# Attention scores as three 64-row terms, the two halves of the keys on the two halves of the rows

## The chip, the cores and the metric

The kernel runs on one core of one Trainium2 chip. The metric is the device time of one execution in microseconds (us). The kernel before takes 1475.3 us, the median of three runs (1474.57 to 1476.85).

## The reference, cut to what matters

Two encoder layers over 1024 tokens of width 1024. In each layer a normalised `x` is projected into two groups of heads: group A is differential attention (4 heads, each with two score maps over 64-wide queries and keys, and a relative-position bias), group B is grouped-query attention (8 query heads on 2 key heads, 64 wide, normalised and rotated). Each group's output is gated, both are concatenated, projected, normalised and added to `x`.

```python
sc = jnp.einsum('cbhqd,cbhkd->cbhqk', qblk, kt).astype(jnp.float32) + bias   # group A, d = 64
p = jax.nn.softmax(sc, axis=-1)
a = p[0] - lam * p[1]
...
sc = jnp.einsum('bgrqd,bgkd->bgrqk', qblk, kt).astype(jnp.float32)           # group B, d = 64
p = jax.nn.softmax(sc, axis=-1).astype(vt.dtype)
```

All values are float32. Every score is a sum over 64 products.

## The kernel before, in words

**Precision.** The matmuls work on float32 tiles of a rounded type (`F32R`). To keep float32 accuracy an operand is split into a rounded part, hi, and the rest, lo, and products are summed: hi·hi, hi·lo and lo·hi in the projections (`mm3`), and in the scores all four products.

**Stages of a layer.** First come the projections (from the start to 312 us in the first layer), which leave queries, keys and values, split, in DRAM tensors (`aq_d`, `ak_d`, `av_d`, `bq_d`, `bk_d`, `bv_d`). Then the attention stage (312 to 627 us in the first layer, 1041 to 1356 us in the second), then the output projection and the normalisation, which in the first layer runs on into the next layer's projections.

**The attention stage.** `all_items` goes through 4 head pairs `h` and 4 token groups `g`; each of these 16 steps has 8 items, 4 of group A and 4 of group B, so 128 items a layer and 256 in all. One item is 128 queries against 1024 keys. `tick` issues one item's work: transposes of an earlier item's probabilities (`pT`, 8 of 128 x 128), the reduction of this item's scores (DVE), the scores of the next item into a tile `pS` of 128 x 1024 (`scores`), some matmuls of probabilities with values (`pO`), the exponential (ACT), then what splits the transposed probabilities into hi and lo. In this stage all four engines execute in the order in which the program is written. `pS` and `pT` have two buffers each.

**The scores.** Rows 0 to 63 of a query tile and of a key tile hold 64 features, and so do rows 64 to 127. For group A the key tile has hi in the upper rows and lo in the lower, and the query tile has the same part in both, so that one matmul over 128 rows gives q·(hi + lo); a second matmul with the queries' lo part adds the other two products. For group B the queries' hi and lo are stacked and the keys doubled. Either way an item has four matmuls: two terms, each on two halves of 512 keys, since a matmul writes 512 columns:

```python
for i in range(2):
    x0 = qi * 512 + i * 256 + c * P
    for kh in range(2):
        n = slice(kh * 512, kh * 512 + 512)
        pe.matmul(pS[:, n], q[:, x0:x0 + P], K[:, c, n], start=(i == 0), stop=(i == 1))
```

**The loads of the stage.** SyncE (SP) issues every DMA, in order. `load_q` fetches the queries of one step (lines 803 to 808), `load_ak` keys of group A and a bias tile (810 to 818), `load_av` values, `load_bk` keys of group B. Their tiles, named `h`, come from a ring of ten buffers, so that a load waits on the SP queue until the tile ten allocations earlier has been read. The queries of a step are requested one step ahead.

**Elsewhere.** `build_bias_rows`, once in the first layer's projections, has the program's only matmuls on 64 rows (`pl[:4]`, 64 rows, 4 stationary columns, 512 columns; named `pO<-e,rbs` in the profile). They run in two visits of two, between projection matmuls into `pS`. Every compute instruction goes through a helper class, so the profile shows them all under its line, L65, and they are told apart by their tiles.

Of the kernel before, what the change touches and what calls it, by code (L numbers as in the profile page):

```python
# [10 lines left out]
F32R = mybir.dt.float32r  # L11
# [6 lines left out]
P = 128  # L18
S = 1024
# [32 lines left out]
def hybrid_encoder(ctx, tc, x, rel_bias, pre_norm_g, w_in, diff_lambda, diff_subln_g,  # L52
                   q_norm_g, k_norm_g, w_out, post_norm_g, onehot, rope, out):
    nc = tc.nc
# [16 lines left out]
    pe, dve, act, gps = Engine(nc.tensor), Engine(nc.vector), Engine(nc.scalar), Engine(nc.gpsimd)  # L71
# [11 lines left out]
    def nm(p):  # L83
        uid[0] += 1
        return f"{p}{uid[0]}"

    def h_tile(shape, dt=F32):
        return sb.tile(shape, dt, tag="h", name=nm("h"), bufs=10)
# [4 lines left out]
    def e_tile(shape=(P, 1024), dt=F32):  # L93
        return sb.tile(list(shape), dt, tag="e", name=nm("e"), bufs=6)
# [7 lines left out]
    def s_tile(n=1, tag="s", bufs=12):  # L102
        return sm.tile([P, n], F32, tag=f"{tag}{n}", name=nm("s"), bufs=bufs)

    def ps_s(shape=(P, 1024), dt=F32):
        return ps.tile(list(shape), dt, tag="S", name=nm("pS"), bufs=2)
# [7 lines left out]
    def d_tile(shape, name):  # L114
        return dr.tile(shape, F32, tag=name, name=name)

    def f(t):
        return t.bitcast(F32)
# [184 lines left out]
    def layer(l, hT, ends, given):  # L303
# [3 lines left out]
        aq_d = d_tile([4, 64, 4, 1024], f"aq_d{l}")  # L307
        ak_d = d_tile([4, 2, P, S], f"ak_d{l}")
        av_d = d_tile([4, P, 2, NT, P], f"av_d{l}")
        bq_d = d_tile([4, P, 4, 512], f"bq_d{l}")  # L310
        bk_d = d_tile([P, 2, 2, S], f"bk_d{l}")
# [275 lines left out]
        def after(delay, fn, mid=False):  # L587
            later_q.append((now[0] + delay, mid, fn))
# [8 lines left out]
        def transpose_unit(e, aT, qi, pool_half):  # L597
            c0 = qi * P
            rest = []
            for kh in range(2):  # L600
                pT = ps_t((P, 4, P))
                for i in range(4):
                    k = kh * 4 + i
                    pe.transpose(pT[:, i, :], e[:, k * P:(k + 1) * P], ident)
                hi = aT[0][:, kh * 4:kh * 4 + 4, c0:c0 + P]
                lo = aT[1][:, kh * 4:kh * 4 + 4, c0:c0 + P]
                if kh == pool_half:
                    full = e[:, kh * 512:kh * 512 + 512].rearrange("p (k c) -> p k c", c=P)
                    act.copy(full, pT)

                    def fin(hi=hi, lo=lo, full=full):
                        gps.tensor_copy(hi, full)
                        gps.tensor_tensor(lo, full, f(hi), ALU.subtract)
                else:
                    act.copy(hi, pT)

                    def fin(hi=hi, lo=lo, pT=pT):
                        dve.tensor_tensor(lo, pT, f(hi), ALU.subtract)
                rest.append(fin)
            return rest  # L620

        def tick(item, nxt):
# [17 lines left out]
            run_later(False)  # L640
            now[0] += 1

        def a_items(q, K, T5, t, qi, aT, r0, out):
            bias = T5[:, 896 - P * t:896 - P * t + 1024]
            es = [None, None]
            sums = s_tile(2, "asum", 4)
            items = []
            for c in range(2):
                def scores(c=c, box=[]):
                    pS = ps_s()  # L650
                    for i in range(2):
                        x0 = qi * 512 + i * 256 + c * P
                        for kh in range(2):
                            n = slice(kh * 512, kh * 512 + 512)
                            pe.matmul(pS[:, n], q[:, x0:x0 + P], K[:, c, n], start=(i == 0), stop=(i == 1))
                    return pS

                def reduce(pS, c=c):
                    es[c] = e_tile()
                    m = s_tile()  # L660
                    dve.tensor_tensor_reduce(out=es[c], in0=pS, in1=bias, op0=ALU.add, op1=ALU.min,
                                             scale=1.0, scalar=3.0e38, accum_out=m)
                    return m

                def expo(pS, m, c=c):
                    act.activation(es[c], es[c], AF.Exp, bias=m, scale=-1.0, accum_out=sums[:, c:c + 1])
                    if c == 1:
                        after(CD, combine)
                items.append((scores, reduce, expo))

            def combine():
                rec = s_tile(2, "arec", 4)
                dve.reciprocal(rec, sums)
                cc = s_tile()
                dve.scalar_tensor_tensor(cc, sums[:, 0:1], neglam, rec[:, 1:2], ALU.mult, ALU.mult)
                dve.tensor_copy(r0[:, qi:qi + 1], rec[:, 0:1])
                a, b = es
                gps.tensor_scalar(b, b, cc, 0.0, ALU.mult, ALU.add)
                gps.tensor_tensor(a, a, b, ALU.add)

                def go():
                    return transpose_unit(a, aT, qi, None) + [lambda: parts.extend(out or [])]
                trans.append((now[0] + AD, go))
            return items
# [44 lines left out]

        def b_items(q, K, j, qi, bT, sr, out):  # L730
            es = []

            def scores():
                pS = ps_s()
                x0 = 1024 + j * 256 + qi * P
                for i in range(2):
                    for kh in range(2):
                        n = slice(kh * 512, kh * 512 + 512)
                        pe.matmul(pS[:, n], q[:, x0:x0 + P], K[:, i, n], start=(i == 0), stop=(i == 1))
                return pS  # L740

            def reduce(pS):
                m = s_tile()
                dve.tensor_reduce(out=m, in_=pS, axis=AX.X, op=ALU.max, negate=True)
                return m

            def expo(pS, m):
                e = e_tile()
                act.activation(e, pS, AF.Exp, bias=m, scale=1.0, accum_out=sr[:, j * 2 + qi:j * 2 + qi + 1])

                def go():
                    return transpose_unit(e, bT[j], qi, PH) + [lambda: parts.extend(out or [])]
                trans.append((now[0] + BD, go))
            return [(scores, reduce, expo)]
# [46 lines left out]
            return [w_tile([P, NK, 256]) for _ in range(2)]  # L801

        def load_q(h, g):
            q = h_tile([P, 1536], F32R)
            for half in range(2):
                nc.sync.dma_start(f(q)[half * 64:half * 64 + 64, :1024], aq_d[h, :, g, :])
            nc.sync.dma_start(f(q)[:, 1024:], bq_d[h, :, g, :])
            return q

        def load_ak(h):  # L810
            K = h_tile([P, 2, S], F32R)
            for i in range(2):
                nc.sync.dma_start(f(K)[i * 64:i * 64 + 64], ak_d[h, i].rearrange("(c p) t -> p c t", p=64))
            T5 = h_tile([P, 1920])
            rows_h = rep_d[h]
            nc.sync.dma_start(T5, bass.AP(tensor=rows_h.tensor, offset=rows_h.offset + 127,
                                          ap=[[2047, P], [1, 1920]]))
            return K, T5

# [4 lines left out]
            nc.sync.dma_start(f(values[h]), av_d[h])  # L824

        def load_bk(kv):
            K = h_tile([P, 2, S], F32R)
            nc.sync.dma_start(f(K), bk_d[:, kv])
            return K

        w_half, half_loads, half_convs = w_steps(w_out[l], 0, on_dve=DVE_OUT)
        state = {"q": load_q(0, 0), "ak": load_ak(0), "bk": load_bk(0)}

        def all_items():
            for h in range(4):
# [6 lines left out]
                if h == 2:  # L842
                    state["bk"] = load_bk(1)
# [44 lines left out]
        while ahead:  # L888
            cur, pS = ahead, held
# [152 lines left out]
    for l in range(DEPTH):  # L1042
        hT, given, ends = layer(l, hT, ends, given)
# [53 lines left out]
```

## Time and profile before

| | |
|---|---|
| median of three runs | 1475.3 us |
| profiled execution: time, span | 1476.72 us, 1474.9 us |
| TensorE matmul (PE) busy | 1440.0 us, 98% of the span |
| DVE, ACT, POOL busy | 843.2, 804.0, 774.2 us |
| attention stages | 312 to 627 us and 1041 to 1356 us, 128 items each |
| score matmuls | 1024, four to an item |
| DMA | 162.47 MB, mean 110 GB/s |

A line of the profile names the engine, the operation, the tile written and the tiles read, the shape and the count; behind the bar stand busy time in us, mean ns of one, and the idle time of the engine before them with what ended it. PE is the stream of matmuls and PEld the stream of weight loads, which put the stationary operand into the array. In the chain of waits a line is a start in us, a duration in us, the engine and tile, and how many instructions were merged; in the timeline the idle time ahead stands in brackets. In the stretches, each engine has its busy time and, in brackets, its instructions.

### The profile page before, as it was taken

Reading aid. Unit: us, or ns where it says so; the run is one execution under the profiler, and the core shown is the slowest. Engines: PE = TensorE matmul, PEld = TensorE weight load, DVE = VectorE, ACT = ScalarE, POOL = GpSimd, SP = SyncE. Lnnn points to the kernel's source line nnn. Section 1 sums busy time; section 2 is a strip of 40 time slices with the busy share of each in tenths; the row PEclk is TensorE's granted clock in tenths of the full one; section 3 lists DMA queues with packets and bytes.
Section 4 is the critical chain, followed back from the end, with each engine's and each line's share of the span. In section 5 each row is a group of like instructions: output and inputs, shape, how many; then the busy total and the mean of one; then the engine's idle time right before and its main releaser. Section 6 shows DMA issues by size and latency. Waiting matters only on the chain.

```text
span 1474.9 us, 22694 instructions
## 1 busy us (share of the span) xinstructions
PE 1440.0 (98%) x8412; PEld 1259.7 (85%) x8412; DVE 843.2 (57%) x1641; ACT 804.0 (55%) x1572; POOL 774.2 (52%) x775
## 2 busy tenths in 40 slices
PE   6999999999999999999899999999999999999998
PEld 6887888888999999988788888888899999999887
DVE  7752110038888888852787500100588888888423
ACT  5443122138888888852444421121588888888321
POOL 4671222018888888852435620120388888888320
PEclk9999999999999999999999999999999999999999
DMA  6467722155324322041334564222653242310303
GB/s 218 120 184 214 244 102 52 29 185 154 106 65 112 88 79 73 2 143 58 132 110 120 171 169 145 86 50 85 183 130 94 51 133 65 94 58 30 115 27 131
DMA packets 109391, 162.47 MB, mean 110 GB/s; under 512 B 7128, under 2 KB 71128, under 8 KB 106976
## 3 DMA queue, kind: packets, MB, share of 16 engines
q1 hardware_dynamic: 109280, 161.02, 36.8%
q8 instruction: 66, 1.08, 0.3%
q14 instruction: 45, 0.37, 0.1%
HBM read 112.72 MB, written 52.46 MB: 112 GB/s over the span
## 4 chain that ended last, share of the span: by engine, by line
PE 86%; issue 4%; DVE 3%; POOL 2%; ACT 1%; DMA 0%; POOLq 0%; DVEq 0%; ACTq 0%
PE pS L65 39%; PE pO L65 34%; PE pT L65 13%; DVE y L65 2%; POOL w L65 1%; DVE h L65 1%; POOL e L65 0%; DVE s L65 0%; ACT e L65 0%; DMA h<-in_w_out_dram 0%; POOL s L65 0%; ACT w L65 0%; ACT o L65 0%; DVE w L65 0%; DVE e L65 0%
## 5 line engine op out<-in xcount | busy, mean ns | idle before, releaser
L65 PE MATMUL pO<-w,h 128*128 128x256 f32 (+1 forms) x3592 | 654.2, 330 | 0.2
L65 PEld LDWEIGHTS pO<-w,h 128*128 128x128 f32 x3592 | 568.3, 189 | 81.5 <-POOL w L65 0.8
L65 PE MATMUL pS<-h,h 128*128 128x512 f32 x1024 | 294.7, 410 | 0.0
L65 POOL TENSOR_TENSOR w<-h,w 128x1024 fp32r<-128x1024 f32 x56 | 136.4, 2453 | 258.0 <-ACT w L65 257.3
L65 PE MATMUL pT<-identr,e 128*128 128x128 f32 x1536 | 200.8, 273 | 1.2 <-DVE w L65 0.9
L65 PEld LDWEIGHTS pS<-h,h 128*128 128x128 f32 x1024 | 174.8, 189 | 24.6 <-ACT e L65 0.4
L65 PE MATMUL pS<-w,h 128*128 128x512 f32 (+1 forms) x912 | 195.5, 371 | 0.0
L65 POOL TENSOR_SCALAR e<-e,s 128x1024 f32<-128x1024 f32 x64 | 71.8, 1122 | 229.8 <-DVE s L65 229.8
L65 DVE TENSOR_TENSOR w<-pT,w 128x512 fp32r<-128x512 f32 x256 | 169.9, 684 | 31.1 <-ACT w L65 30.9
L65 PEld LDWEIGHTS pS<-w,h 128*128 128x128 f32 x912 | 159.9, 191 | 27.6
L65 PEld LDWEIGHTS pT<-identr,e 128*128 128x128 f32 x1536 | 172.6, 140 | 5.7 <-DVE w L65 4.8
L65 PE MATMUL pS<-h,w 128*128 128x512 f32 x768 | 176.8, 390 | 0.0
L65 POOL TENSOR_TENSOR w<-e,w 128x512 fp32r<-128x512 f32 x128 | 168.7, 1318 | 10.4
L65 POOL TENSOR_TENSOR s<-s,mhalf 128x2 f32<-128x2 f32 (+2 forms) x96 | 84.1, 877 | 168.0 <-DVE s L65 164.1
L65 PEld LDWEIGHTS pS<-h,w 128*128 128x128 f32 x768 | 143.4, 188 | 30.4 <-PE pO L65 0.5
L65 ACT CAST w<-pT 128x512 fp32r<-128x512 f32 x256 | 143.7, 587 | 45.8 <-PE pT L65 43.0
L65 DVE TENSOR_REDUCE s<-pS 128x1 f32<-128x1024 f32 x128 | 156.2, 1220 | 16.1 <-PE pS L65 15.2
L65 ACT ACTIVATE e<-e,s 128x1024 f32<-128x1024 f32 x128 | 148.2, 1158 | 22.5 <-DVE s L65 21.8
L65 DVE CUSTOM_DVE_ANT_0 e<-pS,h 128x1024 f32<-128x1024 f32 x128 | 155.5, 1216 | 5.6 <-PE pS L65 4.7
L65 POOL TENSOR_TENSOR e<-e,e 128x1024 f32<-128x1024 f32 x64 | 153.2, 2394 | 5.3
L65 ACT ACTIVATE e<-pS,s 128x1024 f32<-128x1024 f32 x128 | 144.4, 1128 | 7.1 <-issue 5.8
L65 ACT ACTIVATE o<-pO 128x128 f32<-128x128 f32 (+2 forms) x97 | 36.9, 381 | 130.8 <-PE pO L65 115.3
(77 smaller groups left out, 1167.0 us busy)
## 6 DMA issues: line engine op xcount, KB each, us to landing
h<-in_w_in_dram SPq DMA_DIRECT2D x52, 512.0 KB, 5.5
h<-aq_d SPq DMA_DIRECT2D x64, 256.0 KB, 4.8
bq_d<-y SPq DMA_DIRECT2D x32, 256.0 KB, 4.2
aq_d<-e SPq DMA_DIRECT2D x32, 256.0 KB, 4.8
ak_d<-e SPq DMA_DIRECT2D x16, 512.0 KB, 3.0
h<-bq_d SPq DMA_DIRECT2D x32, 256.0 KB, 5.6
h<-ak_d SPq DMA_DIRECT2D x16, 512.0 KB, 9.7
av_d<-e SPq DMA_DIRECT2D x32, 256.0 KB, 2.5
```

The lines of the kernel that those rows point to most:

```text
L65: ins = fn(*args, **kw)
```

## The change

Each item's scores become three products, hi·hi, hi·lo and lo·hi, each over 64 rows only; the product lo·lo is left out. Rows 0 to 63 hold queries and the first 512 keys, rows 64 to 127 the same queries and the other 512 keys. A new function issues the six matmuls of an item, alternating between the upper and the lower rows:

```diff
+        def row_pair_scores(q_of, k_of):
+            pS = ps_s()
+            for n, (iq, ik) in enumerate(((0, 0), (0, 1), (1, 0))):
+                for half in range(2):
+                    rows = slice(half * 64, half * 64 + 64)
+                    pe.matmul(pS[:, half * 512:half * 512 + 512], q_of(iq)[rows], k_of(ik)[rows],
+                              start=(n == 0), stop=(n == 2))
+            return pS
...
         def a_items(q, K, T5, t, qi, aT, r0, out):
...
-                    for i in range(2):
-                        x0 = qi * 512 + i * 256 + c * P
-                        for kh in range(2):
-                            n = slice(kh * 512, kh * 512 + 512)
-                            pe.matmul(pS[:, n], q[:, x0:x0 + P], K[:, c, n], start=(i == 0), stop=(i == 1))
-                    return pS
+                    return row_pair_scores(lambda i: q[:, qi * 512 + i * 256 + c * P:][:, :P],
+                                           lambda i: K[:, i, c, :])
...
         def b_items(q, K, j, qi, bT, sr, out):
...
+                return row_pair_scores(lambda i: q[:, 1024 + i * 512 + j * 256 + qi * P:][:, :P],
+                                       lambda i: K[:, i, :])
...
         def load_q(h, g):
-            q = h_tile([P, 1536], F32R)
+            q = h_tile([P, 2048], F32R)
             for half in range(2):
-                nc.sync.dma_start(f(q)[half * 64:half * 64 + 64, :1024], aq_d[h, :, g, :])
-            nc.sync.dma_start(f(q)[:, 1024:], bq_d[h, :, g, :])
+                rows = slice(half * 64, half * 64 + 64)
+                nc.sync.dma_start(f(q)[rows, :1024], aq_d[h, :, g, :])
+                nc.sync.dma_start(f(q)[rows, 1024:].rearrange("p (i c) -> p i c", i=2),
+                                  bq_d[h, :, g, :].rearrange("(i p) c -> p i c", i=2))
             return q
 
         def load_ak(h):
-            K = h_tile([P, 2, S], F32R)
-            for i in range(2):
-                nc.sync.dma_start(f(K)[i * 64:i * 64 + 64], ak_d[h, i].rearrange("(c p) t -> p c t", p=64))
+            K = h_tile([P, 2, 2, 512], F32R)
+            for half in range(2):
+                for i in range(2):
+                    nc.sync.dma_start(f(K)[half * 64:half * 64 + 64, i],
+                                      ak_d[h, i, :, half * 512:half * 512 + 512].rearrange("(c p) t -> p c t", p=64))
...
         def load_bk(kv):
-            K = h_tile([P, 2, S], F32R)
-            nc.sync.dma_start(f(K), bk_d[:, kv])
+            K = h_tile([P, 2, 512], F32R)
+            for half in range(2):
+                rows = slice(half * 64, half * 64 + 64)
+                nc.sync.dma_start(f(K)[rows], bk_d[rows, kv, :, half * 512:half * 512 + 512])
```

What is stored to DRAM, the transposes, the matmuls with the values, the order of `tick` and the rings of buffers stay as they are. The loaded query tile doubles the rows of group B: each half of the rows now holds both its hi and its lo part. The key tile of group B is half as large, since the doubled copy is no longer read.

More of the change, by code (lines that the diff above doesn't have):

```diff
@@ L649, in scores @@
                 def scores(c=c, box=[]):
-                    pS = ps_s()
-                    for i in range(2):
-                        x0 = qi * 512 + i * 256 + c * P
-                        for kh in range(2):
-                            n = slice(kh * 512, kh * 512 + 512)
-                            pe.matmul(pS[:, n], q[:, x0:x0 + P], K[:, c, n], start=(i == 0), stop=(i == 1))
-                    return pS
+                    return row_pair_scores(lambda i: q[:, qi * 512 + i * 256 + c * P:][:, :P],
+                                           lambda i: K[:, i, c, :])
                 def reduce(pS, c=c):
@@ L733, in scores @@
             def scores():
-                pS = ps_s()
-                x0 = 1024 + j * 256 + qi * P
-                for i in range(2):
[L737 to L740, printed above, removed]
+                return row_pair_scores(lambda i: q[:, 1024 + i * 512 + j * 256 + qi * P:][:, :P],
+                                       lambda i: K[:, i, :])
             def reduce(pS):
@@ L803, in load_q @@
         def load_q(h, g):
-            q = h_tile([P, 1536], F32R)
+            q = h_tile([P, 2048], F32R)
             for half in range(2):
-                nc.sync.dma_start(f(q)[half * 64:half * 64 + 64, :1024], aq_d[h, :, g, :])
-            nc.sync.dma_start(f(q)[:, 1024:], bq_d[h, :, g, :])
+                rows = slice(half * 64, half * 64 + 64)
+                nc.sync.dma_start(f(q)[rows, :1024], aq_d[h, :, g, :])
+                nc.sync.dma_start(f(q)[rows, 1024:].rearrange("p (i c) -> p i c", i=2),
+                                  bq_d[h, :, g, :].rearrange("(i p) c -> p i c", i=2))
             return q
         def load_ak(h):
-            K = h_tile([P, 2, S], F32R)
-            for i in range(2):
-                nc.sync.dma_start(f(K)[i * 64:i * 64 + 64], ak_d[h, i].rearrange("(c p) t -> p c t", p=64))
+            K = h_tile([P, 2, 2, 512], F32R)
[3 more added lines that the diff above has]
+                                      ak_d[h, i, :, half * 512:half * 512 + 512].rearrange("(c p) t -> p c t", p=64))
             T5 = h_tile([P, 1920])
```

## The prediction

> **What bounds the kernel now.** I read the page first, then the busy time by stage, then the chain of waits inside a stage, and last the few places where TensorE already runs a matmul on 64 rows. The page:
>
> ```profile
> span 1474.9 us, 22694 instructions
> PE 1440.0 (98%) x8412; PEld 1259.7 (85%) x8412; DVE 843.2 (57%) x1641; ACT 804.0 (55%) x1572; POOL 774.2 (52%) x775
> ...
> PEclk9999999999999999999999999999999999999999
> ...
> L65 PE MATMUL pS<-h,h 128*128 128x512 f32 x1024 | 294.7, 410 | 0.0
> L65 PEld LDWEIGHTS pS<-h,h 128*128 128x128 f32 x1024 | 174.8, 189 | 24.6 <-ACT e L65 0.4
> ```
>
> The group pS<-h,h is the attention scores and nothing else: 1024 matmuls, four for each of 256 score tiles (2 layers x 128 items). The granted clock is full throughout, so it plays no part below. The two attention stages, by the view of busy time in stretches:
>
> ```profile
> core 0: us, PE busy (x) PEld busy (x) DVE busy (x) ACT busy (x) POOL busy (x), PEclk, DMA share, GB/s
> 312.00:627.00 315.00, 314.34 (x2168) 287.93 (x2167) 269.27 (x535) 269.25 (x538) 252.34 (x282) 1.00 0.32 85
> 1041.00:1356.00 315.00, 314.34 (x2168) 287.93 (x2167) 269.28 (x535) 269.02 (x538) 252.24 (x282) 1.00 0.32 85
> ```
>
> In each stage TensorE is busy 314.34 of 315 us. One item takes 315 / 128 = 2.46 us; DVE and ACT each need 269.3 / 128 = 2.10 us of it. So whatever an item costs TensorE is paid in full if it rises, and is gained in full if it falls, until an item comes near 2.10 us. The chain in the middle of the first stage says what an item is made of:
>
> ```profile
> 480.76 0.87 PE pT L65 x8
> 481.64 0.95 PE pS L65 x4
> 482.59 0.71 PE pO L65 x6
> ...
> 492.94 0.87 PE pT L65 x8
> 493.82 0.93 PE pS L65 x4
> 494.75 0.96 PE pO L65 x8
> ```
>
> Eight transposes, four score matmuls, some value matmuls, with no step of another engine between. The four score matmuls take 0.93 us of the item. That is the term that the change rewrites.
>
> **The change part by part.** *The score matmuls.* Before: four matmuls of 128 rows x 512 columns. After: six of 64 rows x 512, in three pairs; within a pair one uses rows 0 to 63 and writes columns 0 to 511 of pS, the other rows 64 to 127 and columns 512 to 1023. So two things must be priced which the trace hardly shows: whether the two of a pair run at the same time, and what it costs TensorE to go from 128 rows to 64 and back, twice per item, 512 times in all.
>
> The trace has one relative: `build_bias_rows` issues four matmuls with 64 rows and 4 stationary columns, in two visits in the middle of the projection into pS. The chain around the first visit, and TensorE's weight loads at both:
>
> ```profile
> 121.94 3.40 PE pS L65 x15
> 125.34 0.55 PE pO L65 x2
> 125.90 3.17 PE pS L65 x13
> ```
>
> ```profile
> 125.27 0.09 PEld L65 LDWEIGHTS pO<-e,rbs 64*4 64x4 f32 x2 [0.35 <-issue]
> 125.82 0.30 PEld L65 LDWEIGHTS pS<-h,w 128*128 128x128 f32 x2 [0.47 <-issue]
> ```
>
> ```profile
> 136.92 0.09 PEld L65 LDWEIGHTS pO<-e,rbs 64*4 64x4 f32 x2 [0.35 <-issue]
> 137.48 0.30 PEld L65 LDWEIGHTS pS<-h,w 128*128 128x128 f32 x2 [0.47 <-PE pO L65]
> ```
>
> Undisturbed, a matmul of 512 columns costs 3.40 / 15 = 0.227 us. The visit's two cost 0.55 us, 0.10 more than 2 x 0.227. The 13 behind them cost 3.17 us, 0.22 more than 13 x 0.227 = 2.95. One visit therefore costs 0.10 + 0.22 = 0.32 us beyond its work. The weight loads say how: for the 1024 scores the load row of the page has 24.6 us of idle time ahead of it in all, 0.02 us each, so a load runs under the matmul ahead of it; but here it stands idle 0.35 us before the visit and 0.47 us after it, alike at both places; two matmuls lie between 125.27 and 125.82, which at 0.227 us make 0.45 of that 0.55 us. I read this as TensorE finishing what is under way before it takes weights of another row count, and the first matmul behind that then waiting for its own load.
>
> From that row, going to 64 rows and back costs 0.32 us per item. It might be more here: the visit's weights are 4 columns wide, the change's are 128. This row gives the price of a 128-wide load that nothing hides:
>
> ```profile
> 500.29 0.90 PEld L65 LDWEIGHTS pT<-identr,e 128*128 128x128 f32 x8
> ```
>
> With a load's 140 ns, (0.90 - 0.14) / 7 = 0.109 us from one load to the next. Up to two may stand in the open: that of the first matmul of the item, and that of its partner, since the rows never show two loads at once, so that the second of a pair starts 0.11 us late and the whole group ends that much later. That makes 0 to 0.22 us; I take one, 0.11.
>
> The pairs themselves: if the two run together a pair costs 0.227 us, if they run one after the other 0.454 us. No row shows a pair. They share no row of the array's input and no column of pS, so I take 0.227, and keep 0.454 as a rival. The Trainium skill (TensorE: Matmul & The Clock Gate, Part 3: Packing small matmuls) states that such matmuls start about 4 ns apart; by it a pair would be 0.231 us, and no run here shows it yet.
>
> Sum per item: 3 x 0.227 = 0.68, plus 0.32 for going and coming back, plus 0.11 for loads in the open, is 1.11 us, against 0.93: +0.18 us, with ends of 0.68 + 0.32 = 1.00 (+0.07) and 1.22 (+0.29). Times 256: **+46 us, from +18 to +74**. There is no cover for it: TensorE is the engine that is never idle, and DVE and ACT only wait a little longer.
>
> The open point is whether 64 rows by 128 columns pays what 64 by 4 pays. The Trainium skill (TensorEngine Tiling (Array Packing), Tiling Modes, Key Properties) says that a change of tiling mode drains TensorE while a change of tile does not, and lists 64 rows by 128 columns as a mode apart from 128 by 128. By it the 0.32 us are paid here too, once per item and not per pair. The trace bears out that a change costs something, not that the column count is innocent.
>
> *The loads.* Each of 32 q loads gets one more issue and 256 KB more; each K load of the first group four issues instead of two, of the same bytes; each of the second two instead of one, of half the bytes. The tightest place, second layer, by the SP queue, the landing times of those 25 us, and the chain:
>
> ```profile
> 1062.39 1.26 SPq L813 DMA_DIRECT2D h<-ak_d  x2
> ...
> 1064.34 1.31 SPq L806 DMA_DIRECT2D h<-aq_d  x2
> 1065.69 0.64 SPq L807 DMA_DIRECT2D h<-bq_d  x1
> ```
>
> ```profile
> DMA  9930929998999999999899999999999999899993
> ...
> h<-aq_d SPq DMA_DIRECT2D x6, 256.0 KB, 14.0
> ...
> h<-bq_d SPq DMA_DIRECT2D x3, 256.0 KB, 10.3
> ```
>
> ```profile
> 1081.23 0.93 PE pS L65 x4
> ```
>
> The q whose last part is issued at 1065.69 lands near 1065.69 + 10.3 = 1076 (its aq parts at 1064.34 + 14.0 = 1078) and is first used at 1081.2. Two more K issues (1.26 us) and one more q issue (0.64 us) push it by 1.9 us, and 256 KB more at the 235 GB/s of that stretch by 1.1 us: 1081 at worst, just in time, while slower items move the use later by up to 8 x 0.18 = 1.4 us. So nothing, with a tail of a few us, once per layer. SP waits there, and only further loads are queued behind; the cover is the 15 us between issue and use.
>
> The profiled execution took 1476.7 us (span 1474.9, the 1.8 us around it unchanged), 1.4 above the median 1475.3 of the runs. 1476.7 + 46 = 1523 for such an execution, against the median **1521 us**; the case's own range is 1493 to 1549.
>
> **The rivals.** *No price for going to 64 rows (faster).* If the stall at the visits belongs to the 4-column weights, or if a 64-row load can run under a 128-row matmul, an item loses only the fourth matmul: 0.68 to 0.79 us against 0.93, that is -0.25 to -0.14, times 256 -64 to -36 us: 1411 to 1439, at its middle 1425. An item would then be 2.21 to 2.32 us, still above the 2.10 of DVE and ACT, so the gain would come through. It decides from the point where going and coming back cost less than 0.25 us together. For it: within a visit nothing stalls (the two loads lie within 0.09 us, the second under the first matmul). Against it: the stalls are the same at both visits, and they occur on the way back too, where the weights are 128 wide. The 4 ns rule of the first page named above, with nothing for the change of rows, gives -0.24 us per item and is this case.
>
> *The pairs do not overlap (much slower).* Then six matmuls cost 6 x 0.227 = 1.36 us, +0.43 per item or +110 us, 1585; with the 0.32 us on top +0.75, +192 us, 1667. For it: every row of the trace shows matmuls one behind the other. Against it: no two of those could have run together, as all use the same rows. Here the change would not do what it says.
>
> *The price is about half.* If only the waiting remains, with the loads hidden, 0.68 + 0.11 + 0.16 = 0.95 against 0.93: within 13 us of before, 1462 to 1488.
>
> **How the numbers follow.** Forecast (pairs overlap, switching is paid) 0.47; no price 0.25; no overlap 0.15, a little over half of it with the switching on top; half price 0.13. The range goes from 1425, the middle of the faster case, to 1600, beyond the milder case without overlap; left out are half of the faster case (0.12) and the worst one (0.08). Within 0.2% (3 us, about what a measurement of this kernel can tell from no change) only the half-price case can fall: 0.04; of its rest 0.05 goes to faster and 0.04 to slower. Faster: 0.25 + 0.05 = 0.30. Slower: 0.47 + 0.15 + 0.04 = 0.66.
>
> **What would show it.** In the chain, the pS piece of an item: near 1.1 us with x6 if I am right, 0.7 to 0.8 if there is no price, 1.4 or more if nothing overlaps. In the timeline of TensorE, two score matmuls starting within 0.11 us of each other, and pairs 0.23 us apart, show overlap. In the weight loads, an idle stretch of over 0.3 us ahead of each item's first 64-row load and of the first 128-row load behind it shows the switch; none shows the faster case. DVE and ACT keep 269 us of busy time in stages that grow from 315 to near 338 us each. A chain with a DMA into h in it near the start of a stage would show the loads late. Beyond the stages nothing should move; if something does, my attribution is wrong.

## The result and the profile after

The changed kernel takes 1514.7 us (median; 1514.1 to 1515.6) against 1476.0 us for the kernel before, measured beside it: a ratio of 1.0263, with a 95% interval of 1.025 to 1.0276. It is slower by 39 us; 46 were forecast. The profiled execution took 1515.28 us with a span of 1513.5; its granted clock is 0.997, that of the kernel before 0.996, so the clock explains nothing of the difference.

The page of the changed kernel:

```profile
span 1513.5 us, 23784 instructions
PE 1479.0 (98%) x8924; PEld 1200.2 (79%) x8924; DVE 848.3 (56%) x1641; ACT 806.1 (53%) x1572; POOL 771.2 (51%) x775
...
L65 PEld LDWEIGHTS pO<-w,h 128*128 128x128 f32 x3592 | 549.2, 189 | 149.8 <-issue 88.6
...
L65 PE MATMUL pS<-h,h 64*128 64x512 f32 x1536 | 246.7, 426 | 0.0
...
L65 PEld LDWEIGHTS pS<-h,h 64*128 64x128 f32 x1536 | 124.6, 185 | 54.0 <-issue 33.1
```

There are 1536 score matmuls instead of 1024, yet their busy time fell from 294.7 to 246.7 us. Work has gone; the time did not go with it. DVE, ACT and POOL do what they did before to within 6 us, and TensorE is still 98% busy by its matmul records, since the idle stretches below hide under the tails of matmuls.

The score matmuls bound the stage. What writes the score tile in the two stages of the changed kernel (count, shortest, median and longest in ns, first and last start), and in the second stage of the kernel before:

```profile
L65 PE MATMUL pS<-h,h x768: 383/394/503, 313.0 to 647.9; 64*128 64x512 f32 x192
...
L65 PE MATMUL pS<-h,h x768: 383/394/503, 1060.0 to 1395.0; 64*128 64x512 f32 x192
```

```profile
L65 PE MATMUL pS<-h,h x512: 387/397/500, 1040.6 to 1356.4; 128*128 128x512 f32 x171
```

From the first score to the last, a stage took 315.8 us before and takes 334.9 and 335.0 now. 19.1 and 19.2 are 38.3 of the 38.6 us by which the span grew, so nothing outside the two attention stages moved. Per item that is 19.2 / 128 = 0.15 us. The chain of waits in the middle of the first stage shows where it lies:

```profile
495.34 0.89 PE pS L65 x6
496.23 0.91 PE pO L65 x6
497.14 0.89 PE pS L65 x6
498.03 0.91 PE pO L65 x6
498.94 0.87 PE pT L65 x8
499.82 0.91 PE pS L65 x6
```

Before, the four score matmuls took 0.93 us and the six value matmuls behind them 0.71. Now the six score matmuls take 0.89, and the same six value matmuls 0.91. The chain counts a piece from the end of the one ahead of it, so the way into 64 rows stands in the scores' piece (three pairs at 0.227 would be 0.68; 0.21 is the way in) and the way back in the value matmuls' piece (0.91 - 0.71 = 0.20). Together 0.41 us, against 0.25 that the fourth matmul gave back.

The timeline around one item, first the matmuls in two short stretches, then the weight loads (start, duration from the first start to the last end, count, and the idle time ahead in brackets). A count is that of the stretch, not of the item:

```profile
489.24 0.49 PE L65 MATMUL pT<-identr,e 128*128 128x128 f32 x3
489.66 0.51 PE L65 MATMUL pS<-h,h 64*128 64x512 f32 x2
```

```profile
490.00 0.64 PE L65 MATMUL pS<-h,h 64*128 64x512 f32 x4
490.56 0.39 PE L65 MATMUL pO<-w,h 128*128 128x256 f32 x1
```

```profile
489.35 0.14 PEld L65 LDWEIGHTS pT<-identr,e 128*128 128x128 f32 x1
489.66 0.54 PEld L65 LDWEIGHTS pS<-h,h 64*128 64x128 f32 x6 [0.17 <-issue]
490.56 0.30 PEld L65 LDWEIGHTS pO<-w,h 128*128 128x128 f32 x2 [0.37 <-issue]
```

The first two score matmuls, of at most 503 ns each, take 0.51 us together: they start within 0.01 us of each other and run side by side. So do the loads: six of 185 ns within 0.54 us. And the loads stand idle for 0.17 us ahead of the scores here, where transposes precede them (0.13 where value matmuls do), and for 0.37 us behind them. Over the whole run the loads of the scores now wait 54.0 us, before the change 24.6; those of the value matmuls wait 149.8 us, before 81.5.

### The profile page after: what moved, and what is told of

Its sections match the earlier page's. It is cut to its first block, busy times and chain, and to the rows that moved or that the text cites. A ratio compares the mean times of both kernels' runs of the same rounds, so it can differ in the third digit from the quotient of the medians.

```text
span 1513.5 us, 23784 instructions
## 1 busy us (share of the span) xinstructions
PE 1479.0 (98%) x8924; PEld 1200.2 (79%) x8924; DVE 848.3 (56%) x1641; ACT 806.1 (53%) x1572; POOL 771.2 (51%) x775
## 4 chain that ended last, share of the span: by engine, by line
PE 86%; issue 4%; DVE 3%; POOL 2%; ACT 1%; DMA 0%; POOLq 0%; DVEq 0%; SPq 0%; ACTq 0%
PE pS L65 38%; PE pO L65 36%; PE pT L65 12%; DVE y L65 2%; POOL w L65 1%; DVE h L65 0%; ACT e L65 0%; ACT w L65 0%; DVE s L65 0%; POOL s L65 0%; DVE w L65 0%; DMA h<-in_w_out_dram 0%; DMA o<-in_diff_lambda_dram 0%; POOL e L65 0%; DVE e L65 0%
## 5 line engine op out<-in xcount | busy, mean ns | idle before, releaser
L65 PE MATMUL pO<-w,h 128*128 128x256 f32 (+1 forms) x3592 | 679.7, 338 | 0.0
L65 PEld LDWEIGHTS pO<-w,h 128*128 128x128 f32 x3592 | 549.2, 189 | 149.8 <-issue 88.6
L65 PE MATMUL pS<-h,h 64*128 64x512 f32 x1536 | 246.7, 426 | 0.0
L65 POOL TENSOR_TENSOR w<-e,w 128x512 fp32r<-128x512 f32 x128 | 165.3, 1291 | 10.4
L65 PEld LDWEIGHTS pS<-h,h 64*128 64x128 f32 x1536 | 124.6, 185 | 54.0 <-issue 33.1
```

The lines of the kernel that those rows point to most:

```text
L65: ins = fn(*args, **kw)
```

## The experiments

Each compares with the changed kernel's 1514.7 or the kernel before's 1476 to 1477 us. A *visit* is a stretch of 64-row matmuls between 128-row ones. Counted in the order of the programs, the attention stages of the changed kernel have 254 (the first two items of each layer share one).

**e1: the halves apart.** An item's six matmuls in another order.

```diff
-            for n, (iq, ik) in enumerate(((0, 0), (0, 1), (1, 0))):
-                for half in range(2):
+            for half in range(2):
+                for n, (iq, ik) in enumerate(((0, 0), (0, 1), (1, 0))):
```

> The changed kernel with the two loops of an item's six score matmuls exchanged: the three terms of rows 0 to 63 first, then the three of rows 64 to 127. Same matmuls, same loads, same one visit to 64 rows per item. My theory (two matmuls run together only when they stand next to each other in the order and use different rows): only the third and the fourth can pair, so an item takes 5 slots of 0.227 us instead of 3, +0.45 us x 256 = +116 us on 1515, about 1631. Rival (a 64-row matmul is simply cheaper, paired or not, and what costs time is something else in the item): no change, about 1515.

Measured: 1517.4 us, 2.7 more than the changed kernel where my account expected 116. That account, of when two matmuls pair, fell. The rival's reason, that a 64-row matmul is cheaper whether paired or not, is not what the timeline shows either. Two views, of a short stretch and of the whole item:

```profile
489.96 0.51 PE L65 MATMUL pS<-h,h 64*128 64x512 f32 x2
```

```profile
489.96 0.98 PE L65 MATMUL pS<-h,h 64*128 64x512 f32 x6
```

The first two still start together, and all six take 0.98 us (0.97 in the changed kernel), 0.90 us in the chain. In the program the matmuls of rows 64 to 127 now stand behind all three of rows 0 to 63. The trace does not name the rows of a matmul; I read this as two streams, one for each half of the rows, in which a matmul does not wait for those ahead of it that use the other half.

**e4: a fourth pair.** The product of the two lo parts comes back, as in the kernel before.

```diff
-            for n, (iq, ik) in enumerate(((0, 0), (0, 1), (1, 0))):
+            for n, (iq, ik) in enumerate(((0, 0), (0, 1), (1, 0), (1, 1))):
...
-                              start=(n == 0), stop=(n == 2))
+                              start=(n == 0), stop=(n == 3))
```

> The changed kernel with a fourth pair of matmuls per item, the product of the two lo parts, which the kernel before also computed. Measures a pair by itself. My theory (a pair takes as long as one matmul of 512 columns, 0.227 us): +58 us, about 1573. Rival (pairs overlap only in part, or the visit's fixed price hides part of them): more than +75 us, or less than +40 us.

Measured: 1571.2 us, 56.5 more; 56.5 / 256 = 0.221 us for a pair, the price of one 512-column matmul. Two 64-row matmuls overlap completely.

**e2: two visits per item.** The third pair of each item is issued behind the tick's value matmuls.

```diff
...
             if fill:
                 fill.pop(0)()
+            if third:
+                third.pop(0)()
...
+            def pair(n, iq, ik):
...
+            pair(0, 0, 0)
+            pair(1, 0, 1)
+            third.append(lambda: pair(2, 1, 0))
...
```

> The changed kernel with the third pair of every item issued after the value matmuls of the tick, so that nearly every item goes to 64 rows twice. Same matmuls. My theory (each visit to 64 rows costs a fixed 0.40 us, which is what an item of the changed kernel takes beyond three pairs: 0.93 + 0.15 - 0.68): some 246 of 256 items have value matmuls between, so +98 us, about 1613. Rival (the extra time belongs to the item, to its first loads or to the matmuls of values behind it, however often the row count changes): within 10 us of 1515.

Measured: 1583.4 us, 68.7 more, with the same matmuls. The 98 us had a wrong count in them: in ticks without transposes the late third pair stands next to the next item's scores and shares their visit, so there are 432 visits and not 500. The chain shows one such tick, the piece of 0.89 us: three pairs in one visit, of each of which the chain follows one matmul.

```profile
480.12 0.67 PE pS L65 x4
480.78 1.15 PE pO L65 x8
481.93 0.89 PE pS L65 x3
482.82 1.14 PE pO L65 x8
483.96 0.43 PE pS L65 x2
484.40 0.37 PE pO L65 x2
484.76 0.87 PE pT L65 x8
```

178 more visits for 68.7 us make 0.39 us a visit, close to the 0.41 read from the chain. The price hangs on the visit, not on the item.

**e5: the loads alone.** The kernel before with the changed kernel's DMA traffic, or slightly more: the keys of group B keep their full width, 512 KB a load where the changed kernel loads 256.

```diff
-            q = h_tile([P, 1536], F32R)
+            q = h_tile([P, 2048], F32R)
             for half in range(2):
-                nc.sync.dma_start(f(q)[half * 64:half * 64 + 64, :1024], aq_d[h, :, g, :])
-            nc.sync.dma_start(f(q)[:, 1024:], bq_d[h, :, g, :])
+                rows = slice(half * 64, half * 64 + 64)
+                nc.sync.dma_start(f(q)[rows, :1024], aq_d[h, :, g, :])
+                nc.sync.dma_start(f(q)[rows, 1024:].rearrange("p (i c) -> p i c", i=2),
+                                  bq_d[h, rows, g, :].rearrange("p (o c) -> p o c", o=1).broadcast_to([64, 2, 512]))
...
```

> The kernel before with the changed kernel's DMA traffic: the query tile 2048 wide with four loads of 256 KB (the group B part is fetched twice, the second copy is not read), keys of group A in four loads of half rows, keys of group B in two loads of 512 KB. The matmuls are those of before. My theory (the loads are covered by the 15 us and more between issue and use): no change, 1473 to 1479. Rival (part of the +39 us is late loads): 1480 or more.

Measured: 1476.5 us against 1476.8, a ratio of 1.0 with an interval of 0.9991 to 1.001. The loads cost nothing.

**e3: the transposes on 64 rows too.** If the price hangs on the visit, more work in the same visit should be free of it.

```diff
-            for kh in range(2):
-                pT = ps_t((P, 4, P))
-                for i in range(4):
-                    k = kh * 4 + i
-                    pe.transpose(pT[:, i, :], e[:, k * P:(k + 1) * P], ident)
-                hi = aT[0][:, kh * 4:kh * 4 + 4, c0:c0 + P]
+            pTs = [ps_t((P, NK, 64)) for _ in range(2)]
+            for k in range(NK):
+                for half in range(2):
+                    rows = slice(half * 64, half * 64 + 64)
+                    pe.transpose(pTs[half][:, k, :], e[rows, k * P:(k + 1) * P], ident[rows, rows])
+            for kh in range(2):
+                pT = pTs[kh]
+                hi = aT[0][:, :, c0 + kh * 64:c0 + kh * 64 + 64]
...
```

> The changed kernel with the transposes of probabilities done on 64 rows too: 16 half transposes per item, in pairs on rows 0 to 63 and 64 to 127, into two PSUM tiles of 128 x 8 x 64. Where transposes and scores are neighbours, one visit to 64 rows now holds both; the number of visits stays about one per item. My theory (the price is paid at each change of the row count, not by each 64-row group, and two 64 x 128 weight loads run side by side as in the scores): a pair of half transposes takes the 0.109 us of a whole one, the stall moves from before the scores to before the transposes, the time stays within 10 us of 1515. Rival (every group of 64-row matmuls that starts pays for itself): some 192 of 256 items pay 0.2 us or more again, 1553 or more.

Measured: 1478.1 us, 37 faster than the changed kernel and 1.0011 times the kernel before (interval 1.0001 to 1.0021). The rival is out: no second price appears. My own forecast is out too: I had taken a pair of half transposes at 0.109 us, and it is cheaper:

```profile
509.46 0.57 PEld L65 LDWEIGHTS pT<-identr,e 64*128 64x128 f32 x16
...
509.95 0.54 PEld L65 LDWEIGHTS pS<-h,h 64*128 64x128 f32 x6
...
510.83 1.29 DVE L65 TENSOR_TENSOR w<-pT,w 128x512 fp32r<-128x512 f32 x2 [0.94 <-ACT w L65]
510.86 0.78 PEld L65 LDWEIGHTS pO<-w,h 128*128 128x128 f32 x6 [0.37 <-issue]
...
512.17 0.51 PEld L65 LDWEIGHTS pT<-identr,e 64*128 64x128 f32 x14 [0.27 <-DVE w L65]
```

Eight pairs of loads in 0.57 us, a load being 0.14: (0.57 - 0.14) / 7 = 0.061 us a pair. The scores' loads behind them show no idle time, and the value matmuls' loads show the 0.37 us of the way back: one visit. Eight pairs save 8 x (0.109 - 0.061) = 0.38 us in each of 192 transpose units, 74 us; half of it, 37, arrived. The other half became waiting, as far as the views go: here DVE stands 0.94 us until ACT has copied what the transposes left, as all eight blocks now end together, and the next unit's loads then stand 0.27 us until DVE has emptied a tile of pT. In the chain from 330 to 610 us TensorE's steps are 98% in the changed kernel and 83% here; DVE, ACT and POOL hold most of the rest. No view adds the 37 us up, and DVE's waits for ACT are not longer in sum than in the changed kernel (10.4 against 13.8 us in 180 us); what is new is that TensorE comes to wait behind them.

**e7: the transposes alone on 64 rows.** e3's transposes in the kernel before, whose scores stay on 128 rows.

> The kernel before, scores on 128 rows, with the transposes of probabilities alone done on 64 rows in pairs as in e3. Each of 192 transpose units is now a visit to 64 rows of its own. My theory (a visit costs about 0.40 us whatever runs in it, and a unit of 16 half transposes takes 0.50 us instead of 0.87): 192 x (0.50 + 0.40 - 0.87) = +6 us, 1476 to 1488; the 37 us that e3 gains on the changed kernel come from sharing the scores' visit. Rival (half transposes are a gain by themselves): 1440 or less.

Measured: 1481.7 us, 5.1 above its kernel before (ratio 1.0041, 1.0026 to 1.0056). With visits of their own the cheaper transposes gain nothing; in e3 they do, because they ride along. The forecast of +6 came out, but in part by luck, as the chain of a unit shows:

```profile
484.15 0.64 PE pT L65 x16
484.80 1.12 PE pS L65 x4
```

Transposes and scores take 0.64 + 1.12 = 1.76 us, against 0.87 + 0.93 = 1.80 before: 0.04 us less in such a unit and not 0.03 more. With 8 x 0.061 = 0.49 us of pairs, a visit that holds half transposes alone costs 0.64 - 0.49 + 1.12 - 0.93 = 0.34 us here, not 0.40. 192 such units would gain 8 us, and the kernel lost 5; no run shows where the 13 us between them lie.

**e6: the scores ahead of the transposes.** e3 with the issue of the next scores moved in `tick`.

```diff
             rest = []
+            if nxt:
+                nxt()
             if trans and trans[0][0] <= now[0]:
                 rest = trans.pop(0)[1]()
             if item:
                 item[0]()
             run_later(True)
-            if nxt:
-                nxt()
...
```

> e3 (scores and transposes both on 64 rows) with the scores of the next item issued ahead of the transposes in each tick instead of behind them. Same work, same visits. In e3 TensorE needs about 2.35 us per item by its own work and takes 2.45; the transposes wait for DVE to empty both pT buffers. My theory (that wait is what e3 loses, and the scores can fill it): toward 2.37 us per item, 1450 to 1465. Rival (DVE and ACT, in order and at 2.10 us per item, set the pace through other waits): 1470 to 1490.

Measured: 1613.1 us, far above both forecasts. The scores need a buffer of pS, and the exponential that frees it comes late; now the transposes stand in line behind that. From the waits of 180 us in the first stage (engine, tile and engine waited for, total, times, longest), e6:

```profile
ACT w L65 <- PE pT L65: 48.8, 46, 1.6
DVE w L65 <- ACT w L65: 45.3, 46, 1.9
PEld pS L65 <- ACT e L65: 42.2, 30, 1.6
```

That wait for ACT is not among e3's.

**e8: fewer visits by issuing late.** e3, and in ticks without transposes the scores are issued at the tick's end, next to the following tick's transposes: 194 visits instead of 254.

```diff
-            if nxt:
+            apart = not rest and bool(parts or fill)
+            if nxt and not apart:
                 nxt()
...
             run_later(False)
+            if nxt and apart:
+                nxt()
...
```

> e3 (scores and transposes both on 64 rows, transposes first) with one more change: in the ticks that have no transposes, the scores of the next item are issued behind the value matmuls, so that they stand next to the following tick's transposes and share that visit to 64 rows. The program then goes to 64 rows 194 times in the attention stages instead of 254. My theory (a visit costs about 0.39 us, from e2's 68 us for 178 more visits, and TensorE still sets most of the pace): 60 x 0.39 = -23 us on e3's 1478, about 1455. Rival (e3 is already paced by DVE, ACT and the two pT buffers, so that TensorE's gain turns into waiting): within 8 us of 1478.

Measured: 1504.9 us, 27 slower than e3, outside both forecasts. The same 180 us, e3 and then e8:

```profile
DVE s L65 <- PE pS L65: 1.5, 9, 0.2
```

```profile
DVE s L65 <- PE pS L65: 20.9, 18, 1.7
```

DVE, which reduces the scores, now waits for them up to 1.7 us at a time. TensorE saved its visits and handed more than their time to an engine that has little to spare.

**e9: fewer visits without lateness.** e3, but the 64 items whose scores fall in ticks without transposes, the first of each two of group B, are computed as before the change. The attention stages then go to 64 rows 192 times.

```diff
+                x0 = 1024 + j * 256 + qi * P
+                if qi == 0:
+                    pS = ps_s()
+                    for i in range(2):
+                        for kh in range(2):
+                            n = slice(kh * 512, kh * 512 + 512)
+                            pe.matmul(pS[:, n], q[:, x0:x0 + P], K[:, i, n], start=(i == 0), stop=(i == 1))
+                    return pS
+                return row_pair_scores(lambda i, half: q[:, x0 + (i ^ half) * 512:][:, :P],
+                                       lambda i, half: K[:, i, half * 512:half * 512 + 512])
...
```

> e3 (scores and transposes both on 64 rows, transposes first), but the scores that fall in ticks without transposes, the first of each two items of group B (64 of 256), are done as before the change: four products, four matmuls on 128 rows. So no tick goes to 64 rows for scores alone: 194 visits in the program instead of 256, as in e8, but no score is issued later than in e3. The group B keys are loaded as before the change (1 MB in one load), the group B queries in three loads. My theory (those 64 items cost 0.93 instead of 0.68 + 0.40 us, and TensorE's time counts as long as DVE isn't kept waiting): -0.15 x 64 = -10 us on e3's 1478, about 1468. Rival (e3 is paced by the other engines): within 4 us of 1478.

Measured: 1470.8 us (1470.7 to 1471.2), a ratio of 0.9962 to the kernel before with an interval of 0.9948 to 0.9976: 0.4% faster than the kernel before, and 7.3 us faster than e3 where 10 were expected. Its chain:

```profile
485.67 0.91 PE pO L65 x6
486.58 0.93 PE pS L65 x4
487.51 0.70 PE pO L65 x6
488.21 0.69 PE pT L65 x16
488.90 0.58 ACT w L65
489.48 0.02 issue
489.50 1.30 DVE w L65 x2
490.80 0.04 issue
490.85 0.65 PE pT L65 x14
491.50 0.81 PE pS L65 x6
```

A 128-row item (x4) has no price behind it: six value matmuls take 0.70 us, as in the kernel before. Where ACT and DVE now stand in the chain, between two transpose units, TensorE waits for pT's buffers: what is left to gain there is not its work.

## Why the prediction was right

**What bounds the stage.** As said: the stages alone grew, by 38.3 of 38.6 us, and an item's change on TensorE came out in full.

**The pairs.** Taken to overlap wholly at 0.227 us a pair; e4 measures 0.221, and the two of a pair start within 0.01 us of each other. No row of the trace before showed one. That they share no rows and no column of pS was the whole argument; it held, but e1 shows that I did not know how.

**The visit.** The two bias visits of the trace before gave 0.32 us with weights 4 columns wide, and 0 to 0.22 for loads that the 128-wide weights leave in the open, of which I took 0.11. The chain after reads 0.41 in all, so 0.09 for the loads: the partner's load runs beside the first one (six loads within 0.54 us) and costs nothing, which is why the lower half of that term's range held. That I took one load and not two was the middle of the range and no argument, so there is luck in it. The argument that the rows never show two loads at once was a wrong reading: the lines shown with it put two loads of 80 ns each into 0.09 us, and two of 188 ns each into 0.30 us. The starts in the timeline say what the price is made of. The second pair starts 0.34 us behind the first (489.66, 490.00), 0.11 more than a pair takes: the first pair's load in the open. Of the 0.21 us of the way in that leaves 0.10 for the stall. From 490.00 to the first value matmul at 490.56 two pairs (0.45) and 0.11 us pass: the stall of the way back, and 0.09 of its 0.20 are left for a load there.

**Rows, not columns.** That 64 rows by 128 columns pays what 64 by 4 paid was the open point, with a quarter of the chance on the other side. The page of the Trainium skill cited for it (TensorEngine Tiling (Array Packing), Tiling Modes, Key Properties) says that a change of mode drains TensorE and a change of tile does not; the trace agrees on both, with idle loads at the changes of rows (0.17 us into them behind transposes, 0.37 us out of them) and six loads in 0.54 us across the pairs. No run changes the columns alone, so what they cost by themselves is not shown.

**The sum.** 0.68 + 0.32 + 0.11 - 0.93 = +0.18 us per item was forecast, 0.89 + 0.20 - 0.93 = +0.16 is read from the chain, 0.15 is the stage divided by its items. Of the 7 us too many about 5 are the loads' term (0.02 us on 256 items) and about 1 the items that share a visit.

**The loads.** Costed at nothing, and e5 shows nothing.

**The signs.** Two that I named were drawn too simply. I expected the pS piece of the chain near 1.1 us; it is 0.89, since the chain books the way back under the value matmuls. And I expected over 0.3 us of idle loads on both sides; ahead of the scores there are 0.17. There transposes of 0.109 us precede them, and matmuls of 0.227 precede the bias visits; I take the difference to come from that. The stages were to grow to near 338 us and grew to 335.

**Where I was wrong is in the expectations.** e1's account of pairing (in order, next neighbours) fell. e2's count of visits was too high. e3 took 0.109 us for a pair of half transposes that takes 0.061. e7 took 0.40 us for a visit whose chain shows 0.34. e6 and e8 took TensorE for the only pace once its work had shrunk; by the waits, pS's buffers and DVE, at 2.10 us of a 2.46 us item, then held it up.

## What to carry to other kernels

Before cutting work by a matmul of fewer rows, look for a place where the kernel already changes its row count and read what that costs both ways, then divide by how much work one visit holds: here 0.40 us a visit against 0.25 us saved. Such a change pays when neighbours come along into the same visit and items that would need one for themselves stay out, as in e9. And when the bounding engine is busy for 314 of a stage's 315 us and the next ones for 269, a loss on it comes out in full (0.16 us an item in the chain, 0.15 in the stage), but of a gain of 74 us only half arrived (e3).

## What the runs showed of the hardware

Two matmuls on different halves of the rows run wholly side by side (0.221 us a pair of 512 columns), and so do their weight loads. The two halves act as two streams: in e1 the order between them in the program made 2.7 us of 1515. Changing the row count costs about 0.2 us each way around scores (0.21 and 0.20 in the chain; 0.39 us for both by e2), and 0.34 us for both around half transposes alone (e7). A transposition of 64 x 128 took 0.061 us a pair where one of 128 x 128 takes 0.109. Half transposes move half as many columns and load half as many rows, and no run separates the two, so the cause of that stays open.
